# State mixing of a two-layer hybrid trunk: 64 rows per head instead of zero blocks, and the second direction's heads on exchanged partitions

## The chip, the cores and the metric

One core of a Trainium2 chip runs the whole program. The metric is the device time of one execution in microseconds (us). The median of three runs of the kernel before is 2036.54 us (2035.83 to 2040.72).

## The reference, cut to what matters

The program runs two layers of a trunk over 256 context tokens and 512 latent tokens (768 in all, width 1024). The first layer holds attention beside an RWKV-7 state mixing, which runs over the tokens in both directions; the change is in that state mixing. Each of the 8 heads and each direction has a 64x64 state:

```python
def rwkv7_scan(state0, r, w, k, v, kk, a, reverse):
    def step(S, inp):
        r_t, w_t, k_t, v_t, kk_t, a_t = inp
        sa = jnp.einsum('bhvk,bhk->bhv', S, kk_t)
        S = (S * w_t[:, :, None, :] - sa[..., None] * (kk_t * a_t)[:, :, None, :]
             + v_t[..., None] * k_t[:, :, None, :])
        return S, jnp.einsum('bhvk,bhk->bhv', S, r_t)
    ...
    for d, rev in ((0, False), (1, True)):
        yc_d, s_ctx = rwkv7_scan(zero, rc, wc[:, :, d], kc[:, :, d], vc, kkc, ac[:, :, d], rev)
        yl_d, _ = rwkv7_scan(s_ctx, rl, wl[:, :, d], kl[:, :, d], vl, kkl, al[:, :, d], rev)
```

## The kernel before, in words

The scan is done in chunks of 32 tokens. There are 24 chunk steps for each direction, and the two directions (d = 0 and 1) go through them together. The 8 heads are 4 pairs `a` of two heads `h`; the features of head 0 lie on partitions 0 to 63, those of head 1 on 64 to 127 (`HALVES`). A block is 64 tokens, that is two chunks, so there are 12 blocks (`NB`).

- `prepare(b)` loads for each direction of a block the tiles `ar` (the factors that are read with the state, 64 columns for each chunk and head pair, with an identity beside them in columns 64 to 127), `kb` (the factors that write it) and `v` (values, in the tile `vm`). Its part `run()` then makes `z`, all products of `kb` and `ar` of a chunk: 8 matmuls of 128 rows by 128 columns, with 128 moving columns, for each direction. Since two heads share the 128 rows, `kb` is laid into the tile `kbd` block by block beside zeros. Masks on VectorE give from one `z` bank the tile `zk` (triangle without the diagonal) and the first half of `z`; ScalarE copies the second half with a sign. `xv` is the product of `zk` and `v`.
- `ard` holds the columns of `ar` times decay factors `dsel` (a POOL product), for one head in one half of the columns and for the other in the other half, with zeros between.
- `step` is the recurrence: `x` = `ard` times `state` (128 rows, 64 columns), `xs` = `x` + `xv`, `u` = `tt` times `xs` (32x32 tiles, `tt` being the inverse of a triangle that was worked out before the stage and stored in `ttD`), `vu`, `s` = `z` times `vu` (64x64 tiles), and the new `state`.
- `outputs` makes `y` from `ard` and `state` (L1055) and from `z` and `vu` (L1057).
- `attend` is the layer's attention, in the pieces `sc` (scores), `pt` (transposes of the probabilities `prob`) and `po` (times the values). It is emitted between the pieces of the state mixing, to fill TensorE while a step waits.

A matmul that uses fewer than 128 rows or columns gives the place of its tile in the array as `tile_position=(row, column)`. I call rows by columns of the tile the form of a matmul: `z`, `pt` and `sc` have the form 128x128, `po`, `x`, `y` and `xv` 128x64, `s` 64x64, `u` 32x32. In the profile's shapes the form stands with a star (128\*64), and each of these fp32 matmuls but `pt` and `sc` is recorded as two passes (x2 in its counts).

The order on each engine is set when the program is built, by a planner (`tile.TileContext` with a timeline) that takes the instruction that its estimate lets start first; `step` and block 0 stand under `tc.high_priority()`. Every engine then works its list strictly in order. PSUM is shared out in banks: `zy` (two banks, for `z`, `xv`, `y` and `yt`), `ch` (one bank, for `x`, `u`, `s`), `po` one, `pt` two, `sc` one of double size. Loads are issued by SP in the order of its list.

Of the kernel before, what the change touches and what calls it, by code (L numbers as in the profile page):

```python
# [18 lines left out]
P = 128  # L19
# [19 lines left out]
HALVES = (slice(0, 64), slice(64, 128))  # L39

# [36 lines left out]
def constants():  # L77
    f = np.float32
    c = Cols()
    p = np.arange(P)  # L80
    c.add("ident", np.eye(P, dtype=f))
    c.add("ones", np.ones((P, P), f))
    same = (p[:, None] // 64 == p[None, :] // 64).astype(f)
    c.add("blk", same)
    c.add("blk2", (p[:, None] // 64 == np.arange(2)[None, :]).astype(f))
    d = p % 64
    partner = p + np.where(d % 32 < 16, 16, -16)
    perm = np.zeros((P, P), f)
# [10 lines left out]
    head, slot = p // 64, (p // 32) % 2  # L99
    own = (head[:, None] == np.arange(2)[None, :])[:, :, None]  # L100
    for dr in (0, 1):
        isk = slot == dr
        sgn = np.where(isk, 1.0, -1.0).astype(f)
        if dr == 0:
            inc, exc = t[None, :] >= s[:, None], t[None, :] > s[:, None]
        else:
            inc, exc = t[None, :] <= s[:, None], t[None, :] < s[:, None]
        c.add(f"rmask{dr}", (own * inc[:, None, :] * sgn[:, None, None]).astype(f))
        c.add(f"kmask{dr}", (own * (exc & isk[:, None])[:, None, :]).astype(f))
# [115 lines left out]
def tile_trunk(ctx: ExitStack, tc: tile.TileContext, t: dict, out, cc: Cols, pc: Cols):  # L225
# [645 lines left out]
    with ExitStack() as sb:  # L871
# [26 lines left out]
        kbd = [bq.tile([P, 4, 2, P], F32, name=f"kbd{n}") for n in range(3)]  # L898
        ari = [bq.tile([P, 4, 2, P], F32, name=f"ari{n}") for n in range(3)]

# [4 lines left out]
        ard = [br.tile([P, 4, 2, 2, 64], F32, name=f"ard{n}") for n in range(5)]  # L905
        zts = [br.tile([P, 4, 2, P], F32, name=f"z{n}") for n in range(4)]
        for n in range(3):
            zero(kbd[n].rearrange("p a c n -> p (a c n)"), n > 1)
            V.tensor_tensor(out=ari[n].rearrange("p a c n -> p (a c) n")[:, :, 64:128], in0=ident[:, 0:64].unsqueeze(1).to_broadcast([P, 8, 64]),
                            in1=ident[:, 64:128].unsqueeze(1).to_broadcast([P, 8, 64]), op=ALU.add)  # L910
        for n in range(5):
            zero(ard[n].rearrange("p a c s n -> p (a c s n)"), n > 1)
# [4 lines left out]
        A.activation(func=AF.Copy, out=dds[:, 0:7, 1, :], in_=DD[1][:, :, 6::-1].rearrange("p a n -> p n a"))  # L917
        A.activation(func=AF.Copy, out=dds[:, 7:23, 1, :], in_=DD[1][:, :, 23:7:-1].rearrange("p a n -> p n a"))
# [13 lines left out]
        def prepare(b):  # L932
# [5 lines left out]
            for d in (0, 1):  # L938
                n = turn[0]
                turn[0] += 1  # L940
                i, c = blk[d] // 2, P * (blk[d] % 2)
                kb, ar, bd = kbd[n % 3], ari[n % 3], ard[n % 5]
                nc.sync.dma_start(ar[:, :, :, 0:64], arD[d][i][:, :, c:c + P].rearrange("q a (c n) -> q a c n", c=2))
                for h in (0, 1):
                    r = HALVES[h]
                    nc.sync.dma_start(kb[r, :, :, 64 * h:64 * h + 64], kbD[d][i, r, :, c:c + P].rearrange("q a (c n) -> q a c n", c=2))
                    v = vD[64 * blk[d]:64 * blk[d] + 64, h].rearrange("(j q) a e -> q j (a e)", j=2)
                    for j in (0, 1):
                        s = 32 * (2 * h + d)
                        nc.sync.dma_start(vm[d][s:s + 32, j].rearrange("q a e -> q (a e)"), v[:, 1 - j if d else j, :])  # L950
                ld.append((kb, ar))
                ars.append(bd)
                zs.append(zts[n % 4])

            def run():
                zks = {}
                for d in (0, 1):
                    kb, ar = ld[d]
                    for h in (0, 1):
                        r = HALVES[h]  # L960
                        G.tensor_tensor(out=ars[d][r, :, :, :, 32 * h:32 * h + 32].rearrange("p a c s t -> p (a c) s t"),
                                        in0=ar[r, :, :, 0:64].rearrange("p a c (s t) -> p (a c) s t", s=2),
                                        in1=dsel[r, b, d].rearrange("p a c -> p (a c)").unsqueeze(2).unsqueeze(3).to_broadcast([64, 8, 2, 32]),
                                        op=ALU.mult)
                    for m in (0, 1):

                        ps = psum("zy", "z")
                        for a in (0, 1):
                            for c in (0, 1):
                                T.matmul(ps[:, P * (2 * a + c):P * (2 * a + c) + P], lhsT=kb[:, 2 * m + a, c, :], rhs=ar[:, 2 * m + a, c, :],  # L970
                                         start=True, stop=True)
                        pv = ps.rearrange("p (n x) -> p n x", x=P)
                        z = zs[d][:, 2 * m:2 * m + 2].rearrange("p a c x -> p (a c) x")
                        zk = bq.tile([P, 4, 64], F32, tag="zk", name=u("zk"), bufs=4)
                        for dst, c0, nm in ((zk, 32, "kmask"), (z[:, :, 0:64], 0, "rmask")):
                            V.tensor_tensor(out=dst.rearrange("p n (h t) -> p n h t", h=2),
                                            in0=pv[:, :, c0:c0 + 32].unsqueeze(2).to_broadcast([P, 4, 2, 32]),
                                            in1=K(f"{nm}{d}").rearrange("p (h t) -> p h t", h=2).unsqueeze(1).to_broadcast([P, 4, 2, 32]), op=ALU.mult)
                        A.activation(out=z[:, :, 64:128], in_=pv[:, :, 64:128], func=AF.Copy, scale=K(f"sgn{d}"))
                        zks[d, m] = zk  # L980
                        yield
                for j in (0, 1):
                    px = psum("zy", "xv")
                    for a in range(4):
                        for d in (0, 1):
                            c = 1 - j if d else j
                            T.matmul(px[64 * d:64 * d + 64, 64 * a:64 * a + 64], lhsT=zks[d, a // 2][:, 2 * (a % 2) + c, :], rhs=vm[d][:, j, a, :],
                                     start=True, stop=True, tile_position=(0, 64 * d))
# [7 lines left out]
        def step(state, n, win, j):  # L996
# [9 lines left out]
            hd = [(a, d, h) for a in range(4) for d in (0, 1) for h in (0, 1)]  # L1006
            if state is not None:
                px = psum("ch", "x")
                for a in range(4):
                    for d in (0, 1):  # L1010
                        T.matmul(px[64 * d:64 * d + 64, 64 * a:64 * a + 64], lhsT=ars[d][:, a, cl[d], 1, :], rhs=state[:, d, a, :],
                                 start=True, stop=True, tile_position=(0, 64 * d))
# [5 lines left out]
            for a, d, h in hd:  # L1018
                q, w = 2 * d + h, 32 * (2 * h + 1 - d)
                g, k = divmod(NCH * a + idx[d], 32)  # L1020
                T.matmul(pu[w:w + 32, 64 * a:64 * a + 64], lhsT=tt[g][32 * q:32 * q + 32, :, k], rhs=xs[32 * q:32 * q + 32, 64 * a:64 * a + 64],
                         start=True, stop=True, tile_position=(32 * q, w))
# [9 lines left out]
            for d in (0, 1):  # L1032
                for a in range(4):
                    for h in (0, 1):
                        r = HALVES[h]
                        T.matmul(pd[r, 256 * d + 64 * a:256 * d + 64 * a + 64], lhsT=zs[d][r, a, cl[d], 64:128], rhs=vu[d][r, a, :],  # L1036
                                 start=True, stop=True, tile_position=(64 * h, 64 * h))
# [9 lines left out]
        def outputs(state, win, j, vu):  # L1047

            blk, ars, zs, _ = win
            py = psum("zy", "y")  # L1050
            for a in range(4):
                o = [py[64 * d:64 * d + 64, 64 * a:64 * a + 64] for d in (0, 1)]
                if state is not None:
                    for d, c in enumerate((j, 1 - j)):
                        T.matmul(o[d], lhsT=ars[d][:, a, c, 0, :], rhs=state[:, d, a, :], start=True, stop=False, tile_position=(0, 64 * d))  # L1055
                for d, c in enumerate((j, 1 - j)):
                    T.matmul(o[d], lhsT=zs[d][:, a, c, 0:64], rhs=vu[d][:, a, :], start=state is None, stop=True, tile_position=(0, 64 * d))  # L1057
# [731 lines left out]
```

## Time and profile before

| | |
|---|---|
| median of three runs | 2036.54 us |
| the profiled execution | 2032.0 us, its span 2030.2 us, mean granted TensorE clock 0.969 |
| PE, DVE, ACT, POOL busy over the span | 1890.3, 1222.5, 833.7, 380.7 us |
| the state mixing's main part | 387.5 to 648 us |
| DMA over the span | 229.24 MB |

The profile's other parts (the prologue, the projections, the MLPs and the second layer) aren't touched by the change, so the table gives the stretch in which the state mixing runs. "Busy" of PE there counts matmuls from start to their modelled end. A row of a list of waits gives the engine and operation that waited, what it waited for, then us in total, times, and the longest.

### The profile page before, as it was taken

The page shows a single profiled execution, that of the slowest core. Times are in us where ns is not written, and L with a number is a line of the kernel's source. Part 1 is how long each engine was busy: PE and PEld are TensorE (multiplying, and loading weights), DVE is VectorE, ACT ScalarE, POOL GpSimd, SP SyncE. Part 2 cuts the span into 40 slices and gives each one's busy share as a digit, 9 for nine tenths or more (in the row PEclk, how much of TensorE's full clock was granted, in tenths as well). Part 3 has the DMA queues.
Part 4 walks back from the last instruction along what each step waited for, and adds up shares of the span by engine and source line. Part 5 has one row for each costly group of instructions (what it writes and reads, how often), then busy time and mean ns, then how long its engine had stood idle before and what let it go on. Part 6 is the DMA issues. An engine that isn't in the chain of part 4 may idle for free.

```text
span 2030.2 us, 34262 instructions
## 1 busy us (share of the span) xinstructions
PE 1890.3 (93%) x13992; PEld 1546.9 (76%) x13992; DVE 1222.5 (60%) x2077; ACT 833.7 (41%) x1411; POOL 380.7 (19%) x379
## 2 busy tenths in 40 slices
PE   6999977799996999999999999899899789999997
PEld 4777656576675898888888889778668487888886
DVE  5457889776666775555544443865677464344436
ACT  4333333455552543332233224554566444333335
POOL 0032268322222440000000002310153120000002
PEclk9999998799998999999999999999899799999998
DMA  9346565742243742344444432212101133323333
GB/s 322 130 138 206 176 192 151 167 103 48 63 97 96 235 134 84 125 125 135 125 126 130 129 94 73 88 45 73 42 1 43 42 94 95 101 86 103 94 98 110
DMA packets 148173, 229.24 MB, mean 113 GB/s; under 512 B 65056, under 2 KB 102320, under 8 KB 147888
## 3 DMA queue, kind: packets, MB, share of 16 engines
q1 hardware_dynamic: 141200, 214.59, 35.8%
q10 hardware_dynamic: 5456, 7.73, 1.2%
q0 software_dynamic: 1360, 4.73, 0.7%
q8 instruction: 110, 1.80, 0.4%
q14 instruction: 47, 0.39, 0.1%
HBM read 200.53 MB, written 26.48 MB: 112 GB/s over the span
## 4 chain that ended last, share of the span: by engine, by line
PE 72%; DVE 11%; DMA 7%; POOL 3%; ACT 3%; issue 3%; SPq 0%; DVEq 0%; POOLq 0%; ACTq 0%
PE m L367 37%; PE win L367 11%; DMA wmod<-in_wmod_dram 5%; PE po L341 4%; PE pt L332 2%; PE z L970 2%; PE wout L1287 2%; DVE wlo L280 2%; PE wout L1703 1%; PE sc L1132 1%; PE s L1036 1%; DVE junk L1304 1%; PE z L1545 1%; PE mod L405 1%; PE y L1057 1%
## 5 line engine op out<-in xcount | busy, mean ns | idle before, releaser
L279 ACT ACTIVATE whi<-wraw 128x1024 fp32r<-128x1024 f32 x214 | 226.5, 1059 | 681.2 <-PE m L367 561.2
L280 DVE TENSOR_TENSOR wlo<-wraw,whi 128x1024 fp32r<-128x1024 f32 x214 | 264.6, 1237 | 208.5 <-ACT whi L279 205.6
L367 PE MATMUL m<-hh,whi 128*128 128x512 f32 (+1 forms) x816 | 239.3, 344 | 5.0 <-ACT relu L1226 2.3
L367 PE MATMUL m<-hl,whi 128*128 128x512 f32 (+1 forms) x816 | 241.1, 343 | 0.2 <-POOL hl L503 0.2
L367 PE MATMUL m<-hh,wlo 128*128 128x512 f32 (+1 forms) x816 | 241.1, 344 | 0.0
L367 PE MATMUL m<-dl,whi 128*128 128x256 f32 (+1 forms) x832 | 240.7, 341 | 0.0
L367 PE MATMUL m<-dh,whi 128*128 128x256 f32 (+1 forms) x832 | 238.5, 342 | 1.9 <-DVE xl L1208 1.8
L367 PE MATMUL m<-dh,wlo 128*128 128x256 f32 (+1 forms) x832 | 239.9, 341 | 0.1
L471 POOL TENSOR_TENSOR acc<-acc,nsq 128x256 f32<-128x256 f32 x42 | 45.0, 1080 | 868.2 <-ACT nsq L470 867.7
L367 PEld LDWEIGHTS m<-dh,whi 128*128 128x128 f32 x832 | 153.2, 188 | 24.1 <-DVE xl L1208 5.1
L367 PEld LDWEIGHTS m<-hh,whi 128*128 128x128 f32 x816 | 152.1, 188 | 24.7 <-ACT relu L1226 2.7
L367 PEld LDWEIGHTS m<-hl,whi 128*128 128x128 f32 x816 | 153.7, 188 | 19.3 <-POOL hl L503 0.4
L367 PEld LDWEIGHTS m<-dl,whi 128*128 128x128 f32 x832 | 153.8, 188 | 19.0
L367 PEld LDWEIGHTS m<-dh,wlo 128*128 128x128 f32 x832 | 153.6, 188 | 18.8 <-DVE wlo L280 0.3
L367 PEld LDWEIGHTS m<-hh,wlo 128*128 128x128 f32 x816 | 153.5, 188 | 18.9 <-DVE wlo L280 0.3
L367 PE MATMUL win<-hl,whi 128*128 128x512 f32 (+1 forms) x512 | 161.2, 348 | 5.3 <-POOL hl L503 3.5
L367 PE MATMUL win<-hh,whi 128*128 128x512 f32 (+1 forms) x512 | 159.4, 357 | 2.0 <-ACT hh L498 1.9
L367 PE MATMUL win<-hh,wlo 128*128 128x512 f32 (+1 forms) x512 | 158.9, 345 | 0.0
L1304 DVE SCALAR_TENSOR_TENSOR junk<-wmod,crow 128x1024 f32<-128x1024 f32 x64 | 78.5, 1226 | 115.6 <-DMA wmod<-in_wmod_dram 115.0
L1208 DVE SCALAR_TENSOR_TENSOR xl<-m,modT,xl 128x512 f32<-128x512 f32 (+1 forms) x144 | 97.3, 686 | 72.3 <-PE m L367 72.3
L367 PEld LDWEIGHTS win<-hh,whi 128*128 128x128 f32 x512 | 95.5, 194 | 29.5 <-issue 9.7
L367 PEld LDWEIGHTS win<-hl,whi 128*128 128x128 f32 x512 | 98.6, 193 | 21.4 <-POOL hl L503 4.7
(408 smaller groups left out, 3620.6 us busy)
## 6 DMA issues: line engine op xcount, KB each, us to landing
wraw<-in_w_dram SPq DMA_DIRECT2D x136, 512.0 KB, 3.6
wmod<-in_wmod_dram SPq DMA_DIRECT2D x96, 512.0 KB, 4.1
wraw<-in_wout_dram SPq DMA_DIRECT2D x40, 512.0 KB, 3.7
wraw<-in_win_dram SPq DMA_DIRECT2D x35, 512.0 KB, 4.2
arD<-ar SPq DMA_DIRECT2D x8, 768.0 KB, 3.7
kbD<-kb SPq DMA_DIRECT2D x8, 768.0 KB, 4.4
ari<-arD SPq DMA_DIRECT2D x24, 256.0 KB, 4.1
kbd<-kbD SPq DMA_DIRECT2D x48, 128.0 KB, 3.8
```

What stands on the lines that cost most here:

```text
L279: A.activation(out=hi, in_=src, func=AF.Copy)
L280: (lo_eng or V).tensor_tensor(out=lo, in0=src, in1=hi.bitcast(F32), op=ALU.subtract)
L332: T.transpose(pt[:, P * j:P * j + P], prob[j][:, P * m:P * m + P], ident)
L341: T.matmul(po[HALVES[i], :], lhsT=vt[:, k_, r], rhs=w_, start=m_ < 2, stop=m_ + 2 >= n, tile_position=(0, 64 * i))
L367: T.matmul(part(ps, s), lhsT=a[:, c], rhs=row(b, k, s), start=first and j == 0 and q == 0, stop=last and j == n - 1 and q == 2)
L405: T.matmul(ps[r:r + 32, :], lhsT=cs[:, k, :], rhs=wm[:, c], start=k == 0, stop=k == KT - 1, tile_position=(0, r))
L471: (V if k == KT - 1 else eng).tensor_tensor(out=at(acc, s), in0=at(acc, s), in1=at(sq, s), op=ALU.add)
L970: T.matmul(ps[:, P * (2 * a + c):P * (2 * a + c) + P], lhsT=kb[:, 2 * m + a, c, :], rhs=ar[:, 2 * m + a, c, :], start=True, stop=True)
L1036: T.matmul(pd[r, 256 * d + 64 * a:256 * d + 64 * a + 64], lhsT=zs[d][r, a, cl[d], 64:128], rhs=vu[d][r, a, :], start=True, stop=True, tile ...
L1208: V.scalar_tensor_tensor(out=xs, in0=part(ps, s), scalar=mod(l, which, m, s[2]), in1=xs, op0=ALU.mult, op1=ALU.add)
L1287: T.matmul(part(ps, s), lhsT=a[:, c], rhs=like(b, s), start=k == 0 and q == 0, stop=k == KT - 1 and q == 2)
L1304: V.scalar_tensor_tensor(out=junk, in0=wm, scalar=1.0, in1=crow[:, :, v], op0=ALU.mult, op1=ALU.mult, accum_out=modT[:, l, n, v:v + 1])
```

## The change

The zero blocks go. `kbd` becomes `kb` of half the size, `ard` is half as wide, and everything that used 128 rows with zeros in them now uses 64 rows per head. To let four tiles lie on four different places of the array, the two heads of direction 1 change places between the feature side and the side of the chunk rows: head h of direction d has its chunk rows and its state on `HALVES[h ^ d]`. `HD` is the order in which the four pairs (h, d) are issued.

- `z`: for each `m` two banks are taken, one for each direction, and 16 matmuls of 64x64 are written in the order `HD`, instead of 4 of 128x128 for each direction. In all 384 matmuls instead of 192.
- One mask operation for each bank (`zmask`) instead of two; `zk` is gone, and `xv` reads its rows from `z[:, 32:64]`.
- `x`, `y` and `xv` are 64x32 tiles, twice as many as before (x 184 to 368, y 376 to 752, xv 192 to 384 matmuls). In `outputs` the state's part of all four `a` is written ahead of the part of `vu`.
- `s` and `u` keep their number and form, in another order.
- `ard` is loaded by two DMAs of its own for each block and direction, and POOL multiplies it in place, in one operation of 128 partitions instead of two of 64. `kb` is loaded by one DMA instead of two.
- The zeroing of `kbd` and `ard` is gone; the copies to `dds` for direction 1 are four instead of two.

```diff
+HD = ((0, 0), (1, 0), (1, 1), (0, 1))
...
-                for h in (0, 1):
-                    r = HALVES[h]
-                    nc.sync.dma_start(kb[r, :, :, 64 * h:64 * h + 64], kbD[d][i, r, :, c:c + P].rearrange("q a (c n) -> q a c n", c=2))
+                nc.sync.dma_start(kb.rearrange("q a c n -> q a (c n)"), kbD[d][i][:, :, c:c + P])
...
+                for h in (0, 1):
+                    nc.sync.dma_start(bd[HALVES[h ^ d]].rearrange("q a c s t -> q a (c s t)"), arD[d][i, HALVES[h], :, c:c + P])
...
-                    for h in (0, 1):
-                        r = HALVES[h]
-                        G.tensor_tensor(out=ars[d][r, :, :, :, 32 * h:32 * h + 32]..., in0=ar[r, :, :, 0:64]..., in1=dsel[r, b, d]..., op=ALU.mult)
+                    G.tensor_tensor(out=ars[d]..., in0=ars[d]..., in1=dsel[:, b, d]..., op=ALU.mult)
...
-                        ps = psum("zy", "z")
-                        for a in (0, 1):
-                            for c in (0, 1):
-                                T.matmul(ps[:, P * (2 * a + c):P * (2 * a + c) + P], lhsT=kb[:, 2 * m + a, c, :], rhs=ar[:, 2 * m + a, c, :],
-                                         start=True, stop=True)
+                    pz = [psum("zy", "z") for _ in (0, 1)]
+                    for a in (0, 1):
+                        for c in (0, 1):
+                            for h, d in HD:
+                                kb, ar = ld[d]
+                                w = P * (2 * a + c)
+                                T.matmul(pz[d][HALVES[h ^ d], w:w + P], lhsT=kb[HALVES[h], 2 * m + a, c, :], rhs=ar[HALVES[h], 2 * m + a, c, :],
+                                         start=True, stop=True, tile_position=(64 * h, 64 * (h ^ d)))
...
-                        for dst, c0, nm in ((zk, 32, "kmask"), (z[:, :, 0:64], 0, "rmask")):
-                            V.tensor_tensor(out=dst..., in0=pv[:, :, c0:c0 + 32]..., in1=K(f"{nm}{d}")..., op=ALU.mult)
+                        V.tensor_tensor(out=z[:, :, 0:64], in0=pv[:, :, 0:64], in1=K(f"zmask{d}").unsqueeze(1).to_broadcast([P, 4, 64]), op=ALU.mult)
...
-                    for d in (0, 1):
-                        T.matmul(px[64 * d:64 * d + 64, 64 * a:64 * a + 64], lhsT=ars[d][:, a, cl[d], 1, :], rhs=state[:, d, a, :],
-                                 start=True, stop=True, tile_position=(0, 64 * d))
+                    for h, d in HD:
+                        q = 2 * d + h
+                        T.matmul(px[32 * q:32 * q + 32, 64 * a:64 * a + 64], lhsT=ars[d][HALVES[h ^ d], a, cl[d], 1, :], rhs=state[HALVES[h ^ d], d, a, :],
+                                 start=True, stop=True, tile_position=(64 * (h ^ d), 32 * q))
```

The built order moves on TensorE. The first place is one of the steps in the middle of the stage: PE's list from the end of an `x` on. The numbers behind the names count tiles; the last columns are the shape that is written. First before, then of the changed kernel.

```order
L1011 MATMUL x_6045<-state_5976,ard_3291 64x64
L1011 MATMUL x_6045<-state_5976,ard_3287 64x64
L1011 MATMUL x_6045<-state_5976,ard_3291 64x64
L1011 MATMUL x_6045<-state_5976,ard_3287 64x64
L1011 MATMUL x_6045<-state_5976,ard_3291 64x64
L1057 MATMUL y_5978<-vu_5957,z_3293 64x64
L341 MATMUL po_4420<-pts_4566,vtok 64x512
```

```order
L1009 MATMUL x_6402<-state_6272,ard_3290 32x64 x2
L1009 MATMUL x_6402<-state_6272,ard_3289 32x64 x2
L1009 MATMUL x_6402<-state_6272,ard_3290 32x64 x2
L342 MATMUL po_4957<-pts_5081,vtok 64x512
L342 MATMUL po_4957<-pts_5123,vtok 64x512
```

Before, `x`, `y` and `po` follow each other in one form (128x64); now `x` is 64x32 and `po` still 128x64, so there is a change of form between them. Counted over PE's list from the first `s` to the last `y`, the form changes 285 times before and 336 times now.

The second place is PE's list where a block's `z` are made, again before and then now.

```order
L970 MATMUL z_5997<-ari_3276,kbd_3273 128x128
L341 MATMUL po_4420<-pts_4582,vtok 64x512
L332 MATMUL pt_4766<-cst,prob_4615 128x128
L970 MATMUL z_5997<-ari_3276,kbd_3273 128x128 x2
L1132 MATMUL sc_4703<-kh,qs_4603 128x256
```

```order
L971 MATMUL z_6327<-ari_3278,kb_3275 64x128 x3
L1135 MATMUL sc_5311<-kh,qs_4790 128x256
...
L333 MATMUL pt_5381<-cst,prob_5272 128x128
L971 MATMUL z_6328<-ari_3276,kb_3273 64x128 x8
L971 MATMUL z_6365<-ari_3278,kb_3275 64x128 x8
```

The 16 matmuls of a pair of banks do not stand in the order in which they are written: the planner puts the 8 of one direction (z_6328) ahead of the 8 of the other (z_6365). Of the 24 pairs only the first, in block 0, alternates between the directions. The form of `z` was that of `pt` and `sc`, and is now another.

The third place is SP's list just ahead of the stage, where the inverse is stored (`ttD`) and loaded (`tt`).

```order
L773 DMA ttD<-im_2787 128x1024
L773 DMA ttD<-im_2276 128x1024
L1119 DMA qr_3576<-qD 64x8x128 x2
L1119 DMA qr_3954<-qD 64x8x128
L926 DMA tt_3318<-ttD 128x1024
L926 DMA tt_3319<-ttD 128x1024
```

```order
L774 DMA ttD<-im_2276 128x1024
L882 DMA vtok<-vaD 128x768
L886 DMA kraw_3268<-qD 64x768
L926 DMA tt_3312<-ttD 128x1024
...
L774 DMA ttD<-im_2787 128x1024
L1122 DMA qr_3570<-qD 64x8x128 x2
L1122 DMA qr_3997<-qD 64x8x128 x2
L926 DMA tt_3313<-ttD 128x1024
```

The store and the load of one of the two inverses now stand earlier, the other keeps its place, one `qr` load further back.

More of the change, by code (lines that the diff above doesn't have):

```diff
@@ L98, in constants @@
     t = np.arange(32)
-    head, slot = p // 64, (p // 32) % 2
-    own = (head[:, None] == np.arange(2)[None, :])[:, :, None]
+    slot = (p // 32) % 2
     for dr in (0, 1):
@@ L895, in zero @@
                 A.activation(out=x, in_=ident[:, 0:1].to_broadcast([P, x.shape[-1]]), func=AF.Copy, scale=0.0)
-        kbd = [bq.tile([P, 4, 2, P], F32, name=f"kbd{n}") for n in range(3)]
+        kbs = [bq.tile([P, 4, 2, 64], F32, name=f"kb{n}") for n in range(3)]
         ari = [bq.tile([P, 4, 2, P], F32, name=f"ari{n}") for n in range(3)]
@@ L904, in tile_trunk @@
                 zero(vms[d][n].rearrange("p j a e -> p (j a e)"), n)
-        ard = [br.tile([P, 4, 2, 2, 64], F32, name=f"ard{n}") for n in range(5)]
+        ard = [br.tile([P, 4, 2, 2, 32], F32, name=f"ard{n}") for n in range(5)]
         zts = [br.tile([P, 4, 2, P], F32, name=f"z{n}") for n in range(4)]
         for n in range(3):
-            zero(kbd[n].rearrange("p a c n -> p (a c n)"), n > 1)
             V.tensor_tensor(out=ari[n].rearrange("p a c n -> p (a c) n")[:, :, 64:128], in0=ident[:, 0:64].unsqueeze(1).to_broadcast([P, 8, 64]),
                             in1=ident[:, 64:128].unsqueeze(1).to_broadcast([P, 8, 64]), op=ALU.add)
-        for n in range(5):
-            zero(ard[n].rearrange("p a c s n -> p (a c s n)"), n > 1)
         dds = br.tile([P, 2 * NB, 2, 4], F32, name="dds")
@@ L916, in tile_trunk @@
         A.activation(func=AF.Copy, out=dds[:, 0:23, 0, :], in_=DD[0][:, :, 0:23].rearrange("p a n -> p n a"))
[L917 to L918 removed]
+        for r, o in (HALVES, HALVES[::-1]):
+            A.activation(func=AF.Copy, out=dds[o, 0:7, 1, :], in_=DD[1][r, :, 6::-1].rearrange("p a n -> p n a"))
+            A.activation(func=AF.Copy, out=dds[o, 7:23, 1, :], in_=DD[1][r, :, 23:7:-1].rearrange("p a n -> p n a"))
         V.memset(dsel, 1.0)
@@ L1017, in step @@
             pu = psum("ch", "u")
[L1018 to L1022, printed above, removed]
+            for a in range(4):
+                for h, d in HD:
+                    q, w = 2 * d + h, 32 * (2 * (h ^ d) + 1 - d)
+                    g, k = divmod(NCH * a + idx[d], 32)
+                    T.matmul(pu[w:w + 32, 64 * a:64 * a + 64], lhsT=tt[g][32 * q:32 * q + 32, :, k], rhs=xs[32 * q:32 * q + 32, 64 * a:64 * a + 64],
+                             start=True, stop=True, tile_position=(32 * q, w))
             vu = []
@@ L1031, in step @@
             pd = psum("ch", "s")
-            for d in (0, 1):
-                for a in range(4):
-                    for h in (0, 1):
-                        r = HALVES[h]
-                        T.matmul(pd[r, 256 * d + 64 * a:256 * d + 64 * a + 64], lhsT=zs[d][r, a, cl[d], 64:128], rhs=vu[d][r, a, :],
-                                 start=True, stop=True, tile_position=(64 * h, 64 * h))
+            for a in range(4):
+                for h, d in HD:
+                    r = HALVES[h ^ d]
+                    T.matmul(pd[r, 256 * d + 64 * a:256 * d + 64 * a + 64], lhsT=zs[d][r, a, cl[d], 64:128], rhs=vu[d][r, a, :],
+                             start=True, stop=True, tile_position=(64 * (h ^ d), 64 * (h ^ d)))
             new = bp.tile([P, 2, 4, 64], F32, tag="state", name=u("state"), bufs=3)
@@ L1050, in outputs @@
             py = psum("zy", "y")
-            for a in range(4):
[L1052 to L1057, printed above, removed]
+            cl = (j, 1 - j)
+            if state is not None:
+                for a in range(4):
+                    for h, d in HD:
+                        q = 2 * d + h
+                        T.matmul(py[32 * q:32 * q + 32, 64 * a:64 * a + 64], lhsT=ars[d][HALVES[h ^ d], a, cl[d], 0, :], rhs=state[HALVES[h ^ d], d, a, :],
+                                 start=a == 0, stop=False, tile_position=(64 * (h ^ d), 32 * q))
+            for a in range(4):
+                for h, d in HD:
+                    q, r = 2 * d + h, HALVES[h ^ d]
+                    T.matmul(py[32 * q:32 * q + 32, 64 * a:64 * a + 64], lhsT=zs[d][r, a, cl[d], 0:32], rhs=vu[d][r, a, :],
+                             start=state is None and a == 0, stop=a == 3, tile_position=(64 * (h ^ d), 32 * q))
             for d in (0, 1):
```

39 lines of the change are left out of this document (16 added, 23 removed).

## The prediction

> **What bounds the kernel now.** I read the busy time of the engines by stretch first, then the chain of waits of the main stretch, then what TensorE waits for there, then PE's timeline pass by pass. The stretches are the prelude of the state mixing (315 to 387.5 us) and its main part (387.5 to 648); the columns are length, then PE, PEld, DVE, ACT, POOL busy, clock, DMA share, GB/s.
>
> ```profile
> 315.00:387.50 72.50, 50.44 (x303) 41.31 (x302) 62.74 (x116) 24.32 (x50) 46.27 (x56) 0.78 0.72 178
> 387.50:648.00 260.50, 250.54 (x3785) 184.95 (x3784) 179.65 (x413) 141.75 (x273) 72.51 (x66) 0.99 0.31 71
> ```
>
> In the main part PE is busy 250.5 of 260.5 us, so 10 us are all that any other engine can give back; DVE is at 69%, ACT at 54%. The chain of waits of that part agrees: nine tenths of it are PE.
>
> ```profile
> by line: PE z L970 14.8%; PE po L341 14.0%; PE pt L332 11.3%; PE sc L1132 10.9%; PE s L1036 9.5%; PE y L1057 6.7%; PE y L1055 4.6%; PE x L1011 4.4%; PE u L1021 4.1%; PE xv L987 2.9%; issue 2.4%; DVE st L1134 1.9%; DVE vu L1026 1.2%; POOL va
> ```
>
> The mask operations aren't named in it. What PE waited for there (us in total, times, longest):
>
> ```profile
> PE y L1057 <- DVE vu L1026: 3.2, 5, 1.3
> PE xv L987 <- DVE zk L976: 1.0, 2, 0.6
> PE y L1055 <- ACT z L979: 1.0, 2, 0.6
> PE xv L987 <- ACT z L979: 0.9, 2, 0.5
> PE u L1021 <- DVE xs L1014: 0.7, 2, 0.4
> ```
>
> So the sum is one over PE's list: how many passes, how long each holds the array, and what a change of form costs. PE's timeline shows it (start, us, line, operation, form, passes). A group's length holds the last pass's run-out, so I go from start to start.
>
> ```profile
> 480.42 1.15 PE L1036 MATMUL s<-vu,z 64*64 64x64 f32 x32
> 481.49 1.07 PE L341 MATMUL po<-pts,vtok 128*64 128x512 f32 x2
> ...
> 486.36 0.64 PE L1011 MATMUL x<-state,ard 128*64 128x64 f32 x16
> 486.83 1.02 PE L341 MATMUL po<-pts,vtok 128*64 128x512 f32 x2
> ...
> 488.74 1.16 PE L970 MATMUL z<-ari,kbd 128*128 128x128 f32 x8
> 489.83 1.07 PE L341 MATMUL po<-pts,vtok 128*64 128x512 f32 x2
> ...
> 493.06 0.69 PE L987 MATMUL xv<-vm,zk 128*64 128x64 f32 x16
> 493.68 0.44 PE L332 MATMUL pt<-cst,prob 128*128 128x128 f32 x2
> ...
> 494.85 0.68 PE L1021 MATMUL u<-xs,tt 32*32 32x64 f32 x32
> ```
>
> Passes first. `x`, 16 passes between a `y` and a `po` of its own form, holds PE for 0.47 us, 29 ns a pass. `s`, 32 passes, 1.07 us with a change of form at either end: again some 29 ns. `u`, less the run-out of 0.22, 0.46 us over 31 passes, 15 ns: with a quarter of the array's rows and columns four run side by side, with half of either two. `z` stands with a group of 12 passes in the chain of waits (start, us):
>
> ```profile
> 528.18 1.34 PE z L970 x12
> ```
>
> That is 112 ns a pass.
>
> Now a change of form. `xv` has the same 16 passes as `x`, but comes from and goes to `pt` (128x128): 493.06 to 493.68 is 0.62 us against 0.47. One entry and one exit, that is one change each way shared with the neighbours, cost 0.15 us. `z` between `y` and `po` takes 1.09 for 8 passes of 0.112: 0.19 more.
>
> **The change part by part.**
>
> *z.* 384 matmuls of half the rows and columns in place of 192. Were the four places of the array filled at once, 8 passes of the old form would become 16 passes in four rounds, half the time. But as built the 8 matmuls of one direction stand ahead of the 8 of the other, and one direction has two places only (the diagonal ones or the others). Then 16 passes go two by two: 8 rounds of 112 ns, 0.90 us, what the 8 passes of before took. The row of the whole operation:
>
> ```profile
> L970 PE MATMUL z<-ari,kbd 128*128 128x128 f32 x384 | 57.9, 294 | 2.8 <-ACT z L979 2.4 <-ACT xv L990 0.4
> L961 POOL TENSOR_TENSOR ard<-ari,dsel 64x512 f32<-64x512 f32 x48 | 53.5, 1114 | 48.4 <-DMA ari<-arD 22.2 <-PE y L1055 20.2 <-PE sc L1132 4.0
> L979 ACT ACTIVATE z<-z,cst 128x256 f32<-128x256 f32 x48 | 22.6, 472 | 35.6 <-DVE z L976 27.2 <-DVE st L1140 3.6 <-PE z L970 1.9
> L976 DVE TENSOR_TENSOR zk<-z,cst 128x256 f32<-128x256 f32 x48 | 20.2, 420 | 8.4 <-PE z L970 7.9
> L895 ACT ACTIVATE kbd<-cst 128x1024 f32<-128x1024 f32 x2 | 2.0, 1064 | 0.0
> ```
>
> 384 passes by 112 is 43 us, of which the best end would save 21.5 and the order as built saves nothing. I take 0: the order names 23 of 24 pairs.
>
> *x, y, xv.* Twice the passes, a quarter of the array each: at the 15 ns of `u`, 32 passes take the 0.47 us that 16 took. No row has four 64x32 tiles in flight, so the bounds are 15 ns (nothing changes) and 29 ns (two in flight, as for `s`). The passes are 736 for `x`, 1504 for `y`, 768 for `xv`, 3008 in all: 0 to 3008 by 14 ns, +42 us. I take 0, because `x` before shows two tiles on the same rows and other columns at once, and `u` four on different rows. The Trainium skill ("TensorE: Matmul & The Clock Gate", section "Wait — 56ns, not 53.3ns?") has starts never closer than about 25 ns, however small the matmul is. By that rule the 3008 passes would cost 10 ns more each, +30 us as an estimate. The trace disagrees: `u`'s row is 0.68 us with its run-out over 32 passes, 21 ns even so.
>
> *Changes of form.* This is the term that I count on. `x` and `y` no longer share a form with `po`, nor `z` with `pt` and `sc`; `y`, `x` and `xv` now do among themselves. In PE's list from the first `s` to the last `y` the form changes 336 times, 285 before: 51 more. By `xv`'s row 51 by 0.15 is 7.7 us, by `z`'s 51 by 0.19 is 9.7. I take the second, since the new neighbours of `z` and `sc`, `pt` are of its kind. Bounds: nothing, if forms with equal rows don't hold each other up, and 12.8 at 0.25, which is what a group of 64x32 tiles shows earlier in the program, where 48 pairs of passes with 32 columns (half of 58 ns each, 1.39) took 1.64 from start to start:
>
> ```profile
> 142.54 1.71 PE L786 MATMUL ab<-ar,kb 64*32 64x32 f32 x96
> 144.18 0.50 PE L367 MATMUL win<-hl,whi 128*128 128x512 f32 x1
> ```
>
> *DVE and ACT.* 48 operations at 0.42, 20.2 us, leave DVE, off the path but ahead of `vu` and the copies that free `zy` banks. The waits above on `zk` (1.0) end; of the 3.2 on `vu` and the rest of the 10 us perhaps a tenth: I take -2, bounds 0 and -6.8 (the sum of the five rows above). Behind it, PE is late next.
>
> *POOL and the loads.* The 48 products of 1.11 us become 24 with the same 512 columns, 27 us less on an engine that is 28% busy; hidden by PE. `ard` is now loaded, 24 times 256 KB, 6.3 MB more in 260 us at a DMA share of 0.31, which I cost at nothing. The load waits for the last reader of the buffer five tiles back, so SP may stand on `y`, where POOL did (20.2 us in its row). Behind SP then stand the `v` and `qr` loads; SP already waits long for its buffers without PE's waiting for it:
>
> ```profile
> SPq L943 <- PE z L970: 69.7, 17, 12.0
> SPq L950 <- DVE vu L1026: 68.5, 19, 13.7
> ```
>
> The cover is the block of lead, 260.5 / 12 = 21.7 us, against a longest wait of 13.7; without it each block could lose up to the difference of a load's time, some 2 us, 24 us in all. 0 taken.
>
> *The prelude.* It ends when `tt` has landed and `u` of the first step can go:
>
> ```profile
> 316.33 0.98 POOL L893 MEMSET vm<- 128x512 f32 x2
> 317.27 0.95 POOL L893 MEMSET kbd<- 128x1024 f32 x1
> 318.17 2.75 POOL L893 MEMSET ard<- 128x1024 f32 x3
> ...
> 350.66 0.39 DVE L770 TENSOR_TENSOR abm<-abm,it 128x220 f32<-128x220 f32 x1
> ...
> 369.51 1.24 DVE L771 STREAM_TRANSPOSE im<-abm 64x1024 f32<-64x1024 f32 x1
> 370.76 1.93 DVE L772 STREAM_TRANSPOSE im<-abm 64x1024 f32<-64x1024 f32 x1
> ...
> 377.02 1.05 SPq L926 DMA_DIRECT2D tt<-ttD  x2
> ```
>
> DVE bounds it (62.7 of 72.5 us). POOL's zeroing of `kbd` and `ard` (0.95 + 2.75) goes, and four masks by 0.42 leave DVE, 1.7 us. The transposes of the inverse that POOL works out stand earlier on DVE, about where 350.66 is, 3.2 us of work that only moves; there DVE may wait for POOL. I take -1.2, with the ends -3 (masks and part of the zeroing) and +4 (POOL late by as much as its own gain of 3.7).
>
> **The sum.** +9.7 - 2 - 1.2 = +6.5. Against the profiled execution of 2032.0 us that is 2038.5; the median of the runs lies 4.5 above that execution, so 2043.
>
> **The rivals.**
> 1. *Not slower: changes between 64-row forms are free.* Of the 336 changes 60 are between `z`, `s` and the 64x32 tiles. If the array only stops when the row split changes, 276 are left against 285, -9 by 0.19 is -1.7, and with -2 and -1.2 the sum is -5: 2031.5. It decides if the change between two 64-row forms costs under 0.05 us. The entry of 0.25 above, which has 64 rows and 32 columns against 128, says nothing on it.
> 2. *Faster by more: the places of z do fill across the two directions*, at the ends of the groups of 8 or more widely: up to -21.5, 2021.5. Against it stands the strict order.
> 3. *Much slower: two 64x32 tiles on the same rows don't run together*, +42 +6.5: 2085. By the Trainium skill's floor, as above, it would be +30 +6.5, 2073.
> 4. *Slower: the prelude or a load.* DVE stands behind POOL's inverse and `tt` comes 4 us later in place of 1.2 sooner: 2048; with a block or two waiting for `ard` behind SP, up to 2055.
> 5. *No change:* the 10 us of waits close as PE grows (a longer list hides what DVE and ACT owe), -6.8 in place of -2, sum +1.7: 2038.
>
> **How the numbers follow.** About 0.3%, 6.1 us, is what a measurement here can tell from no change: same is 2030.4 to 2042.6. The forecast (its own range 2039 to 2049 from 0.15 to 0.25 a change) gets 0.4, of which 0.1 falls under 2042.6; rival 5 0.15, all same; rival 1 0.2, split between same (0.1) and faster; rival 2 0.05; rival 3 0.07; rival 4 0.13. Slower 0.3 + 0.07 + 0.13 = 0.5, same 0.1 + 0.15 + 0.1 = 0.35, faster 0.15. The range leaves out rivals 2 and 3 and the far end of 1: 2028 to 2056.
>
> **What would show it.** In the trace after: `z` groups of 16 passes at about 0.9 us (half of it: rival 2). 32 passes of `x` at 0.47 us from start to start, plus about 0.15 when `po` follows (0.93: rival 3). PE's busy time in the main part near 258 to 260 us with waits of 8 us or less; no row of waits on a mask; DVE near 160 us there. The first `s` near 386.3. Wrong would be: the first `s` past 389, SP's waits on `ard` with PE waiting for `ari` or `ard`, or `x` to `s` without the 0.15.

## The result, and the profile after

The changed kernel takes 2050.96 us (median of five runs, 2048.18 to 2055.88) against 2035.83 (2030.14 to 2040.72): 1.0082 times the time before, 95% interval 1.0064 to 1.0100. The profiled executions have spans of 2048.5 and 2030.2 us, a difference of 18.3. The forecast of 2043 had the right sign and some two fifths of the size (+6.5 against +15.1 between these medians). The 18.3 us split into three pieces, by the first `s` and the last `y` in TensorE's timeline: the first `s` stands at 386.0 (387.5 before), the last `y` ends at 667.1 (648.0), and what follows takes 1381.4 (1382.2). That is -1.5, +20.6 and -0.8. So the whole loss is in the main part, and there the same view as before, by stretch, says (length, then PE, PEld, DVE, ACT, POOL busy, clock, DMA share, GB/s):

```profile
315.00:386.00 71.00, 49.14 (x377) 39.48 (x377) 55.99 (x112) 20.84 (x48) 33.26 (x40) 0.76 0.81 211
386.00:667.20 281.20, 261.15 (x5604) 178.12 (x5600) 166.34 (x369) 142.19 (x274) 51.79 (x47) 0.98 0.36 84
```

TensorE is busy 10.6 us longer (261.1 against 250.5) and waits 10 us longer (20.0 against 10.0). DVE has its 13 us less, POOL its 21, and TensorE's waits grew all the same. The chain of waits now holds softmax work (`prob`, `st`) among its larger rows; the rows of PE shown add up to 68% of it, against 83% in the line before the change:

```profile
by line: PE po L342 14.0%; PE z L971 11.5%; PE pt L333 10.0%; PE sc L1135 8.4%; PE s L1034 6.5%; PE y L1054 4.7%; ACT prob L1142 4.5%; PE u L1020 4.1%; PE y L1059 3.8%; DVE st L1137 3.5%; issue 3.5%; PE x L1009 2.7%; PE xv L985 2.1%; ACT z 
```

And what TensorE waited for in the main part (us in total, times, longest) names the same place, `sc` waiting for `prob`:

```profile
PE sc L1135 <- ACT prob L1142: 5.5, 9, 1.7
PE pt L333 <- ACT prob L1144: 2.5, 3, 1.1
PE s L1034 <- issue: 1.9, 2, 1.4
PE y L1054 <- DVE oy L1108: 1.6, 1, 1.6
PE y L1059 <- DVE vu L1025: 1.3, 4, 0.5
```

Before, that wait was 1.0 us. Its row is the third of the view from which the prediction shows five, and is not among those five:

```profile
PE sc L1132 <- ACT prob L1139: 1.0, 4, 0.3
```

A second thing shows only in the stretches of 20 us. Before, the granted clock is 1.00 in each of them from 400 to 640 us. After, it isn't:

```profile
400.00:420.00 20.00, 18.13 (x386) 12.02 (x386) 10.75 (x33) 12.34 (x31) 3.08 (x3) 1.00 0.52 104
420.00:440.00 20.00, 16.42 (x322) 11.56 (x322) 10.55 (x25) 12.75 (x25) 3.09 (x3) 0.87 0.63 131
440.00:460.00 20.00, 19.76 (x288) 11.59 (x287) 10.80 (x23) 8.84 (x15) 2.08 (x2) 0.96 0.06 12
...
640.00:660.00 20.00, 16.59 (x508) 13.59 (x507) 12.32 (x28) 4.19 (x9) 7.05 (x5) 0.91 0.04 11
```

In slices of 2 us the clock is 0.50 from 436 to 440 us and again from 644 to 646. The timeline of the first place shows what comes ahead of it (in brackets the wait before a group and its releaser) and what half clock does to the passes: `u`, 0.68 us for 32 passes elsewhere, takes 1.08.

```profile
431.76 0.65 PE L985 MATMUL xv<-vm,z 64*32 64x64 f32 x32 [0.44 <-ACT yacc L1068]
434.10 0.39 PE L1135 MATMUL sc<-kh,qs 128*128 128x256 f32 x1 [1.69 <-ACT prob L1142]
...
435.79 1.08 PE L1020 MATMUL u<-xs,tt 32*32 32x64 f32 x32
436.80 0.69 PE L333 MATMUL pt<-cst,prob 128*128 128x128 f32 x2
```

TensorE had waited 2.1 of the 2.8 us up to 434.10, and the low clock follows within 2 us. So here a wait was paid twice: in itself, and in the slower passes behind it.

### The profile page after: what moved, and what is told of

Its sections match the earlier page's. It is cut to its first block, busy times and chain, and to the rows that moved or that the text cites. A ratio compares the mean times of both kernels' runs of the same rounds, so it can differ in the third digit from the quotient of the medians.

```text
span 2048.5 us, 37946 instructions
## 1 busy us (share of the span) xinstructions
PE 1900.0 (93%) x15880; PEld 1541.3 (75%) x15880; DVE 1207.1 (59%) x2029; ACT 830.8 (41%) x1409; POOL 349.7 (17%) x351
## 4 chain that ended last, share of the span: by engine, by line
PE 76%; DVE 11%; ACT 4%; DMA 3%; POOL 3%; issue 2%; SPq 0%; POOLq 0%; DVEq 0%; ACTq 0%
PE m L368 43%; PE win L368 10%; PE po L342 3%; PE pt L333 2%; PE wout L1290 2%; PE wout L1706 2%; PE z L971 2%; PE sc L1135 1%; PE z L1548 1%; PE s L1034 1%; DVE abm L771 1%; DVE it L769 1%; DVE wlo L281 1%; PE mod L406 1%; DMA wraw<-in_win_dram 1%
```

## The experiments

All kernels compute the whole program. The table holds, for the main part of each profiled execution, its length, TensorE's work and waits, what half clock took (the sum over slices of 2 us of their length times one less the granted clock), the changes of form (counted in the built order, first `s` to last `y`), and `po`: in how many groups its 56 matmuls stand, and its time (from each pass to the start of the next matmul, or to its own end; where an expectation counts groups, it counts both layers'). The ratio is to the kernel before, with its 95% interval; it comes from several executions, the other columns from one, and executions of one kernel lie up to some 10 us apart.

| kernel | length | work | waits | half clock | forms | po groups, us | first s | ratio |
|---|---|---|---|---|---|---|---|---|
| before | 260.5 | 250.5 | 10.0 | 1.3 | 285 | 44, 36.3 | 387.5 | 1 |
| changed | 281.1 | 261.1 | 20.0 | 5.7 | 336 | 42, 42.2 | 386.0 | 1.0082 (1.0064 to 1.0100) |
| e1, z alternating | 294.0 | 263.7 | 30.2 | 17.2 | 332 | 45, 46.9 | 389.9 | 1.0142 (1.0117 to 1.0167) |
| e2, mask back | 274.6 | 249.1 | 25.5 | 4.0 | 313 | 33, 33.5 | 392.2 | 1.0069 (1.0044 to 1.0094) |
| e3, z undone | 265.9 | 258.4 | 7.6 | 1.2 | 320 | 45, 45.2 | 396.0 | 1.0037 (1.0023 to 1.0051) |
| e4, before with z of 64x64 | 277.3 | 264.5 | 12.9 | 1.4 | 337 | 52, 41.2 | 384.4 | 1.0073 (1.0045 to 1.0102) |
| e5, 6 ahead | 278.9 | 265.1 | 13.7 | 4.4 | 345 | 46, 48.2 | 390.5 | 1.0081 (1.0058 to 1.0104) |
| e6, e1 with 2 ahead | 279.4 | 250.5 | 28.9 | 4.8 | 315 | 46, 48.4 | 391.1 | 1.0063 (1.0039 to 1.0088) |
| e7, e1 with 8 ahead | 268.1 | 241.6 | 26.4 | 3.3 | 309 | 40, 40.3 | 389.4 | 1.0030 (1.0014 to 1.0045) |
| e8, before with 6 ahead | 271.4 | 260.9 | 10.5 | 5.0 | 313 | 52, 40.4 | 386.3 | 1.0057 (1.0036 to 1.0077) |
| e9, before, grouped | 259.3 | 248.6 | 10.8 | 2.8 | 220 | 55, 46.7 | 388.1 | 0.9980 (0.9968 to 0.9991) |
| e10, changed, grouped | 259.8 | 227.5 | 32.3 | 8.7 | 222 | 38, 39.3 | 387.6 | 0.9975 (0.9962 to 0.9989) |
| e11, e10 with 2 ahead | 253.6 | 217.5 | 36.1 | 9.1 | 217 | 29, 29.3 | 392.3 | 0.9975 (0.9960 to 0.9989) |
| e12, e9 with po pairs | 256.6 | 232.0 | 24.5 | 7.1 | 197 | 28, 28.5 | 383.5 | 0.9941 (0.9925 to 0.9956) |

A word on `po`, since much hangs on it. Where passes of `y`, `xv` or `x` stand between the two passes of one `po` matmul, its two halves count as two groups. Counted as one place, from its first pass to its end, the kernel before has 39 places and 38.3 us, e4 44 and 43.7, e8 44 and 43.6, e9 50 and 48.9; in the other rows places and groups are the same. A place then takes 0.98 to 1.05 us on average in every kernel, before and changed, whether it holds one matmul or two partners that stand next to each other. So the time of `po` is the number of its places, and grows with the pairs that the order tears apart.

**Four that take the change apart.** e1 holds the 16 `z` matmuls of a pair in an order that alternates between the directions (each behind the one before it on TensorE, an edge without a wait):

```diff
-                            for h, d in HD:
+                            for h, d in ((0, 1), (1, 1), (1, 0), (0, 0)):
...
+                                if zlast:
+                                    tc.add_manual_dep(mm.ins, zlast[0].ins.name, <order only>, reason="z order")
+                                zlast[:] = [mm]
```

> The changed kernel with the 16 z matmuls of a pair of banks held in an order that alternates between the directions (all four 64x64 places follow each other). If four places run at once as soon as the order lets them, the 688 z passes of the main part take 28 ns each in place of 56: -19 us, about 2031 us against 2051. If two tiles on the same rows or columns exclude each other, or the second bank comes so late that the groups are torn apart, no change, 2048 to 2053. If the waits of TensorE (20 us after, 10 before) are set by ACT and DVE, half of the gain is lost to them: about 2041.

It took 2062.59 us, slower than the changed kernel and above all that I had expected. Yet `z` did what was hoped. In the timeline of e1 its groups are half as long, 24 passes in 0.82 us from start to start where the changed kernel had 16 in 1.02:

```profile
513.87 0.89 PE L972 MATMUL z<-ari,kb 64*64 64x128 f32 x24
514.69 0.69 PE L1024 MATMUL u<-xs,tt 32*32 32x64 f32 x32
```

```profile
497.65 1.09 PE L971 MATMUL z<-ari,kb 64*64 64x128 f32 x16
498.67 1.07 PE L342 MATMUL po<-pts,vtok 128*64 128x512 f32 x2
```

The first is e1, the second the changed kernel. Over the main part `z` fell from 44.8 to 34.7 us, and the whole gain went elsewhere: waits 20 to 30 us, half clock 5.7 to 17.2, `po` 42.2 to 46.9. The stretches of e1 show the clock:

```profile
400.00:420.00 20.00, 17.26 (x312) 11.32 (x307) 10.45 (x29) 12.10 (x31) 3.09 (x3) 0.77 0.63 130
...
660.00:680.00 20.00, 14.81 (x544) 12.71 (x542) 10.83 (x22) 2.48 (x6) 4.32 (x3) 0.83 0.02 4
```

ACT's 2.48 us in the second row mark a stretch without attention: in e1 the last `sc` stands 5 steps earlier than in the kernel before, and the last steps of the recurrence have nothing to fill them.

e2 puts a second mask operation on DVE (its result isn't read):

```diff
+                        zk = bq.tile([P, 4, 64], F32, tag="zk", name=u("zk"), bufs=4)
+                        V.tensor_tensor(out=zk..., in0=pv[:, :, 32:64]..., in1=K(f"zmask{d}")..., op=ALU.mult)
```

> The changed kernel with a second mask operation per bank on DVE again (48 by 0.42 us, 20 us of DVE work whose result nobody reads). Theory: the added 10 us of waits come from the order, since a freer DVE lets the planner run the attention ahead at the start of the stage, faster than ACT works it off; with the mask back the attention is spread as before, waits go back to 10 to 12 us, form changes 336 to 313: 2038 to 2044 us. Rival: the waits come with the longer list or with ACT itself; then DVE work can only cost: 2051 to 2056.

2048.73 us: between my range and the rival's. Waits didn't fall, they rose to 25.5, so the freer DVE alone doesn't explain them; the edit moved the built order too, so it isn't a test of DVE's load by itself. TensorE's work fell by 12 us, of which `po` is 8.7, at 33 places in place of 42. That pointed at `po`.

e3 undoes `z` alone: full tiles from `kb` with zero blocks, two loads, four buffers zeroed.

```diff
-                                T.matmul(pz[d][HALVES[h ^ d], w:w + P], lhsT=kb[HALVES[h], 2 * m + a, c, :], rhs=ar[HALVES[h], 2 * m + a, c, :],
-                                         start=True, stop=True, tile_position=(64 * h, 64 * (h ^ d)))
+                                T.matmul(pz[d][:, w:w + P], lhsT=kb[:, 2 * m + a, c, :], rhs=ar[:, 2 * m + a, c, :], start=True, stop=True)
```

> The changed kernel with z alone undone: 128x128 tiles from kb with zero blocks (four buffers of it, zeroed in the prelude), all else as changed. Form changes 336 to 320. If forms cost 0.19 us each and z costs the same in both: about -3, 2048 us. If the 64x64 form of z itself is the dear part (more weight loads, torn groups): 2040 or less. If the x, y, xv tiles cost nothing: near 2036.

2042.18 us, between two of the cases. Its first `s` comes at 396.0, 10 us later than in the changed kernel and 8.5 later than before, and why stays open. Its main part is 265.9, only 5.4 over before. Waits are 7.6 and half clock took no more than before. Against before its work is +7.9. Six places of `po` more (45 against 39) at 1.0 us are 6 of it; all the rest, with 35 more changes of form, is 1.9, 0.05 each.

e4 does the reverse, the kernel before with `z` alone as 64x64 tiles on the diagonal:

```diff
+                                for h in (0, 1):
+                                    T.matmul(ps[HALVES[h], ...], lhsT=kb[HALVES[h], 2 * m + a, c, HALVES[h]], rhs=ar[HALVES[h], 2 * m + a, c, :],
+                                             start=True, stop=True, tile_position=(64 * h, 64 * h))
```

> The kernel before with z alone as 64x64 tiles on the two diagonal places, all else as before. Passes 384 to 768, two at a time: the same time. Form changes 285 to 337. By 0.19 us each +10, 2046 us; if a change between forms costs nothing, 2036.

2046.58 us, the number expected by 0.19 a change, though not by that alone: in the profiled execution the main part is 16.8 us longer, with 2.9 more of waits, and the first `s` 3.1 earlier. Work is +14.0: `z` itself +3.8, `pt` +3.4, `po` +4.9 in the table, the others together +1.9. Five places of `po` more (44 against 39) at 1.0 us leave 9.0 over 52 changes, 0.17 us each.

**Four on where the attention stands.** e5 is the changed kernel with fewer attention pieces written ahead, e6 and e7 are e1 with the same edit, e8 is the kernel before with it.

```diff
-        for _ in range(40):
+        for _ in range(6):
```

> The changed kernel with 6 in place of 40 pieces of the attention written ahead of the state mixing, nothing else; as built the last scores stand two steps later than in the changed kernel, one step earlier than before, and the form changes 345 times (336 in the changed kernel). Theory: the attention runs ahead and leaves the first steps waiting for the softmax and the last ones without filler; spread again, TensorE's waits fall from 20 us to 10 to 13 and the time at half clock (5.7 us lost, 1.3 before) to 1 to 2; with 9 form changes by 0.19 more the sum is -8 to -12: 2039 to 2043 us. Rival: the waits belong to the finer tiles and stay: 2051 to 2054.

> The kernel with alternating z (four places at once) and 2 in place of 40 attention pieces written ahead; the last scores stand in step 20 as in the kernel before, form changes 315 (332 with alternating z alone). With alternating z alone the main part had 263.7 us of TensorE work, of which some 16 were lost to half clock, and 30 us of waits. Theory: with the attention spread, some 248 us of work at full clock, less 17 changes by 0.19, and 10 to 13 us of waits, a main part of 255 to 259 against 260.5: 2027 to 2034 us. Rival: the second bank of a pair is what is waited for, and the waits stay near 25 us: 2045 or more.

> The same with 8 pieces ahead: last scores in step 18, form changes 309. By the theory between: 12 to 18 us of waits, part of the last steps without filler and at half clock: 2032 to 2044 us. If the place of the attention doesn't matter, as the one with 2 ahead.

> The kernel before with 6 in place of 40 attention pieces written ahead: the same tiles and the same work, in an order with 313 form changes in place of 285. If a change of form costs 0.15 to 0.19 us: +4 to +5.5, 2038 to 2040 us against 2034; if the time comes from the tiles' own passes and not from changes: 2034, less what a later end of the attention saves in waits (up to -3).

e5: 2052.3 us, as the rival said, though the waits fell to 13.7, almost as the theory said. What they gave (6.3) was taken by `po` (+6.0) and by the first `s`, 4.5 later. e6, 2049.52 us, missed: waits stayed at 28.9 and the time in the rival's range. e7, 2042.7, fell in its range by the work (241.6), not by its waits (26.4). e8, 2047.49, was to be 2038 to 2040. Its work is +10.4, of which up to 3.7 are half clock and 5 are the five places of `po` more (44 against 39); 5.3 us more lie behind the main part, where `wout` waits 14.1 us for its input (12.1 before). Of the work 1.7 us remain over 28 changes, 0.06 each. So the price of a change of form comes out as 0.05 (e3), 0.06 (e8) and 0.17 (e4), and these kernels don't settle it. Where the attention stands explains the waits in part only: the same edit took 6.3 us of waits from the changed kernel (e5), 1.3 from e1 (e6), and none from the kernel before (e8). And e8 shows how much an order alone can do: with every tile as before it is 0.57% slower.

**Four that group.** In e9 to e12 the matmuls of one `z`, `xv` or `y` are held together: the first takes its place in the planner's order, the rest follow at high priority behind it, and `y` starts with the part that needs `vu`. In e10 and e11 the 16 `z` matmuls of a pair of banks are one group, written so that the four places follow each other.

```diff
+        def group():
+            last = []
+            def mm(*x, **k):
+                if last:
+                    with tc.high_priority():
+                        i = T.matmul(*x, **k)
+                    tc.add_manual_dep(i.ins, last[0].ins.name, <order only>, reason="run")
+                else:
+                    i = T.matmul(*x, **k)
+                last[:] = [i]
+            return mm
```

> The kernel before, with the matmuls of one z bank, one xv and one y held together: after the first of a group the rest have high priority and stand behind it, and y begins with the part that needs vu. Same tiles, same passes, form changes 220 in place of 285. At 0.24 to 0.27 us a change (kernels with 28 and 52 more changes than before showed this): 65 changes are -16 to -18 in TensorE's work; waits grow from 10 us by what the finer mixing hid, 0 to 6: 2019 to 2026 us. If the changes are not what costs, 2032 to 2040.

> The changed kernel with the same grouping, z alternating between the directions (four places at once, 16 matmuls together). Form changes 222 (336 in the changed kernel). 114 by 0.25 is -28, z -10 to -19, TensorE's work in the main part 261 down to 215 to 225; then waits on the softmax and the recurrence take over, 20 to 40 us: main part 245 to 260 against 260.5 before, 2018 to 2038 us. If the grouping only turns into waits, 2048 or more.

> The same with 2 in place of 40 attention pieces written ahead, so that the attention lasts to the last steps as in the kernel before; form changes 217. By the theory that the attention must last, fewer waits and less half clock at the end than with 40: 2012 to 2030 us. If its place doesn't matter, equal to the one with 40.

e9: 2031.96 us, short of its 2019 to 2026. `y` fell from 35.3 to 25.6, but `po` rose from 36.3 to 46.7: 50 places in place of 39. e10: 2030.31 and e11: 2029.78, both within what was expected. The last kernel is e9 with the two `po` of a pair next to each other (and those of the second layer):

```diff
-                for i, (m_, k_, w_) in enumerate(pair):
-                    T.matmul(po[HALVES[i], :], ...)
+                for i, (m_, k_, w_) in list(enumerate(pair))[::-1]:
...
+                    with tc.high_priority():
+                        mm = T.matmul(po[HALVES[i], :], ...)
+                    tc.add_manual_dep(mm.ins, first.ins.name, <order only>, reason="pair")
```

> The kernel before with its z, xv and y grouped (as in the earlier kernel of that kind, 2032 us) and the two po matmuls of a pair held next to each other too, here and in the second layer's attention. A po pair lies on the two column halves, and two in a row run side by side: the grouped kernel had 81 groups for 92 po and 46.7 us of po in the main part, the kernel before 70 and 36.3; now 48 groups. Theory: the missing gain of the grouped kernel (its TensorE work fell by 2 us where 16 were expected) went to po pairs torn apart; with pairs together po takes some 26 us, the form changes 197 times, TensorE's work is 222 to 230 us, waits grow from 11 to 20 to 30: main part 245 to 257, 2018 to 2030 us. Rival: the softmax and the recurrence hold the stage at 255 to 260 us whatever TensorE does, as in the grouped changed kernels with 32 to 36 us of waits: 2028 to 2034.

2023.08 us (2016.53 to 2024.69), 0.9941 times the kernel before: `po` 28.5 us as the theory said, work 232.0, a little over its range, waits 24.5. It beats both kernels, and it has the tiles of the kernel before. Not all of that is the main part: of the 10.1 us that its profiled span is shorter than before, 4.0 are an earlier first `s`, 3.9 the main part and 2.2 what follows. Against e9 its work in the main part fell by 16.6 us, and 13.7 of that came back as waits. With 256.6 us the main part lies where the rival had it (255 to 260); the total fell below the rival's range by what lies around it. Its timeline shows a pair of `po` (4 passes) in the time that two passes take when they stand alone in e9; the second fence is e9.

```profile
486.56 1.03 PE L341 MATMUL po<-pts,vtok 128*64 128x512 f32 x4
487.52 0.66 PE L332 MATMUL pt<-cst,prob 128*128 128x128 f32 x4
```

```profile
490.56 1.07 PE L341 MATMUL po<-pts,vtok 128*64 128x512 f32 x2
491.56 0.88 PE L332 MATMUL pt<-cst,prob 128*128 128x128 f32 x6
```

And the main parts of e10 and e12 side by side, e10 first:

```profile
387.60:647.30 259.70, 227.44 (x5609) 159.79 (x5609) 162.32 (x363) 140.99 (x274) 51.27 (x46) 0.97 0.39 95
```

```profile
383.50:640.10 256.60, 232.04 (x3787) 180.69 (x3788) 178.00 (x409) 142.01 (x276) 71.58 (x65) 0.97 0.34 78
```

## Why the prediction was right, and where it was not

- **Nine tenths of the chain are PE: too high.** The rows of PE that the prediction shows add up to 83%, so other engines held a sixth of the chain already before.
- **z, 0 of a possible -21.5: right, and shown.** `z` took 44.8 us in both kernels. That the order and not the array withholds the gain is shown by e1 (34.7) and e10 (27.3, with whole groups of 16).
- **x, y, xv at 15 ns a pass: right.** `x` in the changed kernel takes 0.58 us from start to start for its 32 passes, between a `pt` and a `po`: the 0.47 of the sum and 0.11 for the changes, 18 ns a pass with everything in. Over the main part `x`, `y` and `xv` together took 62.2 us before and 62.5 now, counted like `po` in the table. The Trainium skill ("TensorE: Matmul & The Clock Gate", section "Wait — 56ns, not 53.3ns?") states a floor of about 25 ns from start to start. The trace disagrees for these tiles on different places, with its 18 ns.

```profile
500.26 0.65 PE L1009 MATMUL x<-state,ard 64*32 64x64 f32 x32
500.84 1.07 PE L342 MATMUL po<-pts,vtok 128*64 128x512 f32 x2
```

- **Changes of form, +9.7: the total of TensorE's work came near (+10.6), but by luck; its make-up is another.** A part of it is `po`, for which the sum had no term: 42 places and 42.2 us in place of 39 and 38.3, so +3.9, of which the three places more are 3. The rest of it is the entry: a place that follows `y`, `x` or `xv`, which were of its own form before, takes some 0.95 us and not 1.00. In five of the 39 places passes of `y` or `xv`, 11 in all, even start while a pass of `po` runs, and the place takes no longer (0.95 us from 512.95 to 513.90):

```profile
512.95 0.59 PE L341 MATMUL po<-pts,vtok 128*64 128x512 f32 x1
513.00 0.22 PE L1057 MATMUL y<-vu,z 128*64 128x64 f32 x1
513.38 0.59 PE L341 MATMUL po<-pts,vtok 128*64 128x512 f32 x1
513.90 0.33 PE L332 MATMUL pt<-cst,prob 128*128 128x128 f32 x1
```

Without the three places 7.6 of the 10.6 us are left, and half clock took up to 4.4 of them. What remains, 3.2 to 7.6, is 0.06 to 0.15 us for each of the 51 changes; e3, e8 and e4 give 0.05, 0.06 and 0.17. All lie under the 0.19 that I took.
- **Waits, -2: the step that failed.** They grew by 10.0. I had taken a longer TensorE list and a freer DVE to close waits, with bounds of 0 and -6.8 that left no room for a growth. 7.0 of the 10.0 are waits for `prob` (5.5 and 2.5 in the list above, 1.0 before), a row that my list had passed over. The order has a part in it: the attention runs ahead in the first steps (one of the first five steps holds 18 `sc` passes where before none of the first nine holds over 8, and the last `sc` stands three steps earlier), so `sc` waits for `prob` early and the recurrence has less to cover it late. Spreading the attention took 6.3 us of the waits away in e5, but 1.3 in e6, so the rest of the growth stays open; e2 shows that putting DVE's load back doesn't lower them.
- **Half clock: left out.** It took 5.7 us of the main part in place of 1.3, +4.4.
- **The prelude, -1.2: right here (-1.5)**, but a matter of the built order: over the kernels the first `s` lies between 383.5 and 396.0, and in the changed kernel `u` waits 4.0 us for `tt` (1.5 before).
- **POOL and the loads, 0: right.** No wait of TensorE on `ari` or `ard` is among its longer ones; POOL waits 58 us for `ard` to land, which nobody feels:

```profile
L959 POOL TENSOR_TENSOR ard<-ard,dsel 128x512 f32<-128x512 f32 x24 | 27.2, 1139 | 87.6 <-DMA ard<-arD 58.4 <-PE s L1034 12.1 <-PE z L971 11.3
```

Compared under the same grouping, no cost of the change is seen: e10 against e9 is 2030.31 to 2031.96, intervals of 0.9962 to 0.9989 and 0.9968 to 0.9991 against before. There it takes 21 us off TensorE's work (248.6 to 227.5) and gets as much back in waits (10.8 to 32.3). Those 21 us aren't the tiles' alone: `z`, which alternates in e10, is 27.3 us against 42.8, and `po` has 38 places against 50. So the +0.8% isn't a price of the new tiles as such; it goes with the order that the planner built around them, of which the places of `po` and a part of the waits are shown. The missing gain lies in the stage's other bound: with TensorE's work at 217 to 232 us, e10, e11 and e12 all wait 24 to 36 us, at `prob` and in the chain of `u`, `vu`, `s`, and their main parts stay at 254 to 260 us. What TensorE waited for most in e11 (but for 10.8 us of `yt`, behind the last `y`), and then in e12:

```profile
PE sc L1151 <- ACT prob L1158: 9.1, 9, 2.6
PE u L1035 <- DVE xs L1027: 5.2, 6, 1.8
PE x L1024 <- DVE state L1057: 5.2, 7, 1.3
```

```profile
PE s L1057 <- DVE vu L1047: 7.8, 6, 2.1
PE xv L947 <- DVE zk L996: 3.6, 3, 2.1
PE sc L1154 <- ACT prob L1161: 3.1, 7, 1.2
```

In e12, which keeps the second mask, the waits are on DVE; in e11 the softmax leads. Which would have to be shortened first wasn't tried.

## What to carry to other kernels

Packing a matmul into four places gains only if tiles on different places stand next to each other in the engine's built list; read that list, and hold a group together with edges if the planner doesn't. The same holds for two half-wide matmuls: `po` took the same time for a pair as for one alone, so count in the built list how many pairs are torn apart before blaming the tiles. A new form changes the order of everything around it, and here an order moved the time by 0.6% either way with no tile changed (e8, e12), against the 0.8% of the change. A saving on the bound engine shows only as far as the next bound, and waits that it opens can cost more than themselves through the clock.

## What the hardware showed that I had not expected

- In the place shown the clock falls to half within 2 us after 2.1 us of waits in a stretch of 2.8. It stays there for some time: in slices of 2 us, 436 to 440 us in the changed kernel, 412 to 424 in e1, where 17.2 us went that way in all.
- Two matmuls of 128x64 on the two column halves run side by side: 4 passes of 512 columns in 0.96 us, 2 passes of one alone in 1.00.
- Four 64x64 tiles run at once: in e1 24 passes of 128 columns in 0.82 us, 34 ns each with a change of form in it, where two at a time took 64 (16 in 1.02).
